# A gate/up unit's seventh product listed between the next unit's second and third products

## The chip, the cores and the metric

The kernel runs on one NeuronCore of a Trainium2 chip. The metric is device time in microseconds (us), the time of one execution on that core. The shown time of the kernel before is the median of three runs. One further execution was profiled, and every trace row in this document comes from such a profiled execution.

The engines are named as in the profile: PE is TensorE's matmul, PEld its weight load, DVE is VectorE, ACT is ScalarE, POOL is GpSimd, SP is SyncE, which issues the loads here. ACT and DVE each have one queue of instructions.

## The reference

The program is a trunk of two layers over 512 tokens of width 1024. Layer 0 mixes tokens by a stick-breaking attention, layer 1 by a gated MLP over positions. After each mixer stands a SwiGLU feed-forward part with 2816 hidden channels, and only this part matters here:

```
def swiglu(h, w_gate, w_up, w_down):
    return (jax.nn.silu(h @ w_gate) * (h @ w_up)) @ w_down
```

Everything is float32, and norms, shifts, scales and gates stand around each part.

## The kernel before

**Precision.** Each operand of a float32 product is split into a high part and a low remainder. `mm3` (L105) makes one product of two split operands from three matmuls: high by high, high weights by low activations, low weights by high activations. So in the trace `r<-hTh,wh`, `r<-hTl,wh` and `r<-hTh,wl` are the three matmuls of one step. `split` (L113) makes the two parts: ACT copies the high part (L117) and DVE subtracts it for the low part (traced as L70, since all DVE calls but those of plain weights go through a wrapper; those have L162).

**The gate/up stage.** The hidden width is 22 blocks of 128 channels. `units` (L1136) computes them for each of the two feed-forward parts: blocks 0 to 2 by plain sums (`unit`, L1065), and blocks 3 to 21, 19 of them, by `seven` (L1089). A seven unit takes gate and up of its block, two halves of the tokens (lo, hi) and two halves of the 1024 inner channels as a 2x2 by 2x2 block product, and computes it with seven block products in place of eight. Each product is 4 steps of `mm3`, so 12 matmuls of 128x128 weights by 256 tokens; a unit has 84. The products and what reads them, in the order of the listing:

| product | operands | accumulates in | then |
|---|---|---|---|
| 1 | A11 (hT), B11 | R1, fresh | ACT copies R1 to s1 (L1112) |
| 2 | A12 (hT), B21 | R2, fresh | DVE: gate lo = R2 + s1 |
| 3 | S1, T1 | R3, fresh | ACT copies R3 to s5 (L1116) |
| 4 | S2, T2 | R1, added | ACT copies R1 to u1 (L1118) |
| 5 | S4, B22 | R3, added | DVE: up lo = R3 - u1 |
| 6 | S3, T3 | R1, added | DVE: up hi = s5 - R1 |
| 7 | A22 (hT), T4 | R1, added | ACT: Silu of gate lo in place (L1126), Silu of R1 to gate hi (L1127); DVE: act = gate * up |

Row 7 of the table is the inner function `rest` (L1124), which `seven` returns. Product 7 adds into the same bank R1 that "up hi" has just read, so its first matmul has to wait for that DVE instruction. In the trace that instruction is `gu<-e,r`, and "gate lo" and "up lo" are `gu<-r,e`. A12 by B21 is seen as `r<-hTh,b` and `r<-hTl,b`, products 3 to 6 are `r<-Sh,wh`, `r<-Sl,wh`, `r<-Sh,wl`, and products 1 and 7 are both `r<-hTh,wh`, `r<-hTl,wh`, `r<-hTh,wl`.

**Weights.** `wget` (L235) hands out the next unit's weights and first emits the loads and splits of those up to one unit further. `block_loads` (L175) loads 512 KB for rawx and 512 KB for rawy; `blocks` (L186) splits them into x (holding B11, B22), b (B21), t13 (T1, T3) and t24 (T2, T4), with the sums f13 and f24 made by DVE. The split tiles live in six places, three to a unit, so the tiles of unit f+2 take over the places of unit f: its t24 can be split only when product 7 of unit f has read the old one. f24 has one buffer, f13 and b have two. The matmul banks of tag "b" are six, three to a unit.

**What orders the work.** In this stage no order is written out by hand. The listing goes to a scheduler that makes each engine's order at compile time: of the instructions that it reckons ready it takes the one that stands earliest in the listing. Each engine then runs its own order without skipping. So a place in the listing is a rank, not a place on the engine.

**Beside the units** a background generator (`Bg`, L335) loads rows of a modulation matrix and adds them up on DVE, one step (`bg0.step(1)`) after two of each three units, seen as `G<-rawada,sc,G`; its end is two 512-wide matmuls for each half of a row, `adaps`. After the stage, part 0 goes on to the down projection (`out_proj`, matmuls `y`) and part 1 to `last` (matmuls `X`, `Y`, `Z`, `W`).

Of the kernel before, what the change touches and what calls it, by code (L numbers as in the profile page):

```python
# [31 lines left out]
def trunk(ctx: ExitStack, tc: tile.TileContext, A: dict, out: bass.AP):  # L32
# [17 lines left out]
    def nm(s):  # L50
        uid[0] += 1
        return f"{s}_{uid[0]}"

    def slot(dt, name, a=2, b=512):
        return s4.tile([P, a, b], dt, tag="s4", name=nm(name))

    def bank(name, tag="b"):
        return psum.tile([P, 512], F32, tag=tag, bufs=6 if tag == "b" else 2, name=nm(name))
# [46 lines left out]
    def mm3(o, lh, ll, rh, rl, start, stop):  # L105
        mm(o, lh, rh, start, False)
        mm(o, lh, rl, False, False)
        mm(o, ll, rh, False, stop)
# [126 lines left out]
    def wget(src, look=3):  # L235

        n = taken[0]
        taken[0] += 1
        while len(got) < min(n + 1 + look, len(stream)):
            wemit()  # L240
        assert stream[n][3] == src, (stream[n][3], src)
        return got[n]
# [176 lines left out]
    def hB(hT, k, lo, n):  # L419

        h, l = hT[lo // 256, k // 4]
        lo %= 256
        return h[:, k % 4, lo : lo + n], l[:, k % 4, lo : lo + n]
# [630 lines left out]
    class Ffn:  # L1054
# [31 lines left out]
        def first(self):  # L1086
            return [lambda f=f: self.unit(f, 0, 256, 2) for f in range(NH)]

        def seven(self, f):  # L1089

            W = wget(("blocks", (self.li, f - NH)), 1)
            R1, R2, R3 = [bank(n)[:, :256] for n in ("r1", "r2", "r3")]
            S = {n: (lambda k, t=self.S[n]: (t[0][:, k, :], t[1][:, k, :])) for n in "1234"}
            S["A11"] = lambda k: hB(self.hT, k, 0, 256)
            S["A12"] = lambda k: hB(self.hT, k + 4, 0, 256)
            S["A22"] = lambda k: hB(self.hT, k + 4, 256, 256)

            def product(o, a, b, start, stop):
                for k in range(4):
                    h, l = S[a](k)
                    wh, wl = W[b](k)
                    mm3(o, wh, wl, h, l, start and k == 0, stop and k == 3)

            e = fpool.tile([P, 3, 256], F32, tag="e", name=nm("e"))
            gu = npool.tile([P, 2, T], F32, tag="n", name=nm("gu"))
            lo, hi = slice(0, 256), slice(256, T)
            s1, u1, s5 = [e[:, i, :] for i in range(3)]  # L1110
            product(R1, "A11", "B11", True, False)
            act.activation(s1, R1, AF.Copy)  # L1112
            product(R2, "A12", "B21", True, True)
            dve.tensor_tensor(gu[:, 0, lo], R2, s1, ALU.add)
            product(R3, "1", "T1", True, False)
            act.activation(s5, R3, AF.Copy)  # L1116
            product(R1, "2", "T2", False, False)
            act.activation(u1, R1, AF.Copy)  # L1118
            product(R3, "4", "B22", False, True)
            dve.tensor_tensor(gu[:, 1, lo], R3, u1, ALU.subtract)  # L1120
            product(R1, "3", "T3", False, False)
            dve.tensor_tensor(gu[:, 1, hi], s5, R1, ALU.subtract)

            def rest():  # L1124
                product(R1, "A22", "T4", False, True)
                act.activation(gu[:, 0, lo], gu[:, 0, lo], AF.Silu)  # L1126
                last_act[0] = act.activation(gu[:, 0, hi], R1, AF.Silu)  # L1127
                if f // 2 == len(self.act):
                    self.act.append(slot(F32, "act"))
                dve.tensor_tensor(  # L1130
                    self.act[f // 2][:, f % 2, :], gu[:, 0, :], gu[:, 1, :], ALU.mult
                )

            return rest

        def units(self, bg0):  # L1136
            for f in range(NH):
                self.unit(f, 256, 256)()
            for f in range(NH, KF):
                self.seven(f)()  # L1140
                if f % 3:
                    bg0.step(1)
            bg0.step(99)

        def run(self, bg0, bg, bg2, steps, nhT, nxt, nS=None):
            self.units(bg0)
# [5 lines left out]
        def last(self, bg0):  # L1152
# [102 lines left out]
            for q in range(2):  # L1255
# [4 lines left out]
                for n, p in enumerate(PAIRS[q]):  # L1260
                    W = wget(("wdn", q, p), 2)
                    now = O
                    if n + 1 < NF or q == 0:
                        O = operands(*((q, PAIRS[q][n + 1]) if n + 1 < NF else (1, PAIRS[1][0])))
                    if p in SEVEN[q]:
                        seven(now, W, banks, fresh)
                        if p == [i for i in PAIRS[q] if i in SEVEN[q]][-1]:
                            us = common(banks)
                    elif q == 1 and n >= NF - NLAST:
                        tail.append((p, now, W))  # L1270
                    else:
                        for s in range(2):
                            eight(p, now, W, banks, s, (0, 1), ("X", s) in fresh)
                            fresh -= {("X", s), ("Y", s)}
                    if q == 1 and n == NF - NLAST - 2:
                        sqrt_table()
                        xs = [x_load(tt) for tt in range(NT)]
# [277 lines left out]
```

## Time and profile before

| | us |
|---|---|
| three runs | 1136.39, 1134.57, 1135.93 |
| their median | 1135.93 |
| the profiled execution, its own time | 1133.95 |
| its span, from the first to the last instruction | 1132.2 |
| mean granted TensorE clock, as a share of full speed | 0.998 |

| engine | busy us | instructions |
|---|---|---|
| PE | 1110.9 | 7436 |
| PEld | 999.9 | 7436 |
| DVE | 933.0 | 1223 |
| ACT | 596.6 | 985 |
| POOL | 29.5 | 53 |

A timeline row reads: start in us from the span's start, duration in us, engine, line, operation, output and inputs by tile name, shapes, and how many records were merged; in brackets the idle time before it and what ended it. A row of grouped instructions ends with the count, the busy time, the mean duration in ns, and the idle time before. The end of a matmul is modelled and overlaps the next one, so the distance between two starts is what a matmul costs; a stall shows as a longer distance, often without any bracket. The seven units of part 0 stand at about 314 to 507 us, those of part 1 at about 818 to 1012 us.

### The profile page before, as it was taken

What the parts mean: (1) busy time and instruction counts of PE and PEld (TensorE: products, weight loads), DVE (VectorE), ACT (ScalarE), POOL (GpSimd) and SP (SyncE); (2) the same over time, 40 slices, a digit from 0 to 9 for tenths busy, and PEclk for the clock granted to TensorE, in tenths of its full rate; (3) what the DMA queues carried; (4) which work ended last, traced back from release to release, by engine and by line L of the source; (5) the groups of instructions that cost most, each with busy time, mean ns of one, the idle gap of its engine ahead of it and who ended that gap; (6) DMA issues with size and microseconds to landing.
All of it is one profiled execution on the core that took longest, in us unless ns stands there. A gap on an engine that the chain in (4) does not pass through costs nothing.

```text
span 1132.2 us, 18659 instructions
## 1 busy us (share of the span) xinstructions
PE 1110.9 (98%) x7436; PEld 999.9 (88%) x7436; DVE 933.0 (82%) x1223; ACT 596.6 (53%) x985; POOL 29.5 (3%) x53
## 2 busy tenths in 40 slices
PE   6999999999999999999999999999999999999997
PEld 4787878788999999998888988988999999999996
DVE  4988999958989898778686865759979898789996
ACT  6445655656655555572153624537455555465752
POOL 0120100000000000010000100001000000000000
PEclk9999999999999999999999999999999999999999
DMA  8876434214344343348886483324243434223242
GB/s 322 336 238 213 147 98 134 93 59 158 122 150 131 128 151 117 129 136 310 269 275 218 150 280 110 131 94 160 83 132 115 164 130 146 70 85 99 90 154 106
DMA packets 51356, 176.39 MB, mean 156 GB/s; under 512 B 6074, under 2 KB 9146, under 8 KB 51268
## 3 DMA queue, kind: packets, MB, share of 16 engines
q1 hardware_dynamic: 48708, 166.81, 43.6%
q0 software_dynamic: 2560, 8.39, 2.0%
q8 instruction: 58, 0.95, 0.3%
q14 instruction: 30, 0.25, 0.1%
HBM read 164.69 MB, written 8.39 MB: 153 GB/s over the span
## 4 chain that ended last, share of the span: by engine, by line
PE 88%; DVE 5%; ACT 3%; DMA 2%; issue 1%; SPq 0%; DVEq 0%; ACTq 0%
PE r L94 32%; PE y L94 16%; PE v L94 8%; PE pqk L94 7%; PE X L94 4%; PE gu L94 4%; PE Y L94 3%; PE u L94 3%; PE av L94 2%; PE z L94 2%; PE tw L102 1%; PE Z L94 1%; PE W L94 1%; PE tp L102 1%; PE ab L94 1%
## 5 line engine op out<-in xcount | busy, mean ns | idle before, releaser
L94 PE MATMUL r<-Sh,wl 128*128 128x256 f32 x608 | 170.0, 280 | 0.0
L94 PE MATMUL r<-Sh,wh 128*128 128x256 f32 x608 | 169.9, 279 | 0.0
L94 PE MATMUL r<-Sl,wh 128*128 128x256 f32 x608 | 169.8, 279 | 0.0
L161 ACT ACTIVATE wh<-raw 128x1024 fp32r<-128x1024 f32 x87 | 91.6, 1059 | 113.3 <-PE y L94 57.5
L94 PE MATMUL y<-wh,as 128*128 128x512 f32 x480 | 150.7, 391 | 0.0
L117 ACT ACTIVATE wh<-f 128x1024 fp32r<-128x1024 f32 x87 | 92.3, 1061 | 91.3 <-PE r L94 66.4
L70 DVE TENSOR_TENSOR wl<-f,wh 128x1024 fp32r<-128x1024 f32 x87 | 106.4, 1222 | 38.9 <-ACT wh L117 38.8
L162 DVE TENSOR_TENSOR wl<-raw,wh 128x1024 fp32r<-128x1024 f32 x87 | 105.8, 1221 | 38.2 <-ACT wh L161 37.5
L94 PEld LDWEIGHTS r<-Sl,wh 128*128 128x128 f32 x608 | 114.2, 188 | 0.0
L94 PEld LDWEIGHTS r<-Sh,wl 128*128 128x128 f32 x608 | 114.2, 188 | 0.0
L94 PEld LDWEIGHTS r<-Sh,wh 128*128 128x128 f32 x608 | 114.1, 188 | 0.0
L94 PEld LDWEIGHTS y<-wh,as 128*128 128x128 f32 x480 | 90.1, 188 | 18.6
L94 PE MATMUL y<-wl,as 128*128 128x512 f32 x240 | 93.8, 391 | 0.0
L94 PE MATMUL r<-hTh,wh 128*128 128x256 f32 x304 | 88.9, 293 | 0.6 <-DVE gu L70 0.6
L94 PE MATMUL r<-hTl,wh 128*128 128x256 f32 x304 | 84.8, 279 | 0.0
L94 PE MATMUL r<-hTh,wl 128*128 128x256 f32 x304 | 80.0, 279 | 0.0
L94 PEld LDWEIGHTS r<-hTh,wh 128*128 128x128 f32 x304 | 57.0, 188 | 5.9 <-DVE gu L70 2.4
L94 PE MATMUL r<-hTh,b 128*128 128x256 f32 x304 | 59.8, 279 | 0.0
L117 ACT ACTIVATE wh<-rawx 128x1024 fp32r<-128x1024 f32 x38 | 40.3, 1061 | 33.4 <-PE r L94 30.8
L94 PEld LDWEIGHTS r<-hTl,wh 128*128 128x128 f32 x304 | 57.2, 188 | 0.1
L94 PEld LDWEIGHTS r<-hTh,wl 128*128 128x128 f32 x304 | 55.0, 188 | 0.0
L94 PE MATMUL gu<-hTh,wh 128*128 128x256 f32 x192 | 54.0, 281 | 0.0
(272 smaller groups left out, 2960.7 us busy)
## 6 DMA issues: line engine op xcount, KB each, us to landing
rawada<-in_ada SPq DMA_DIRECT2D x80, 512.0 KB, 4.9
rawy<-in_wy SPq DMA_DIRECT2D x38, 512.0 KB, 3.5
rawx<-in_wx SPq DMA_DIRECT2D x38, 512.0 KB, 4.1
raw<-in_wdown SPq DMA_DIRECT2D x22, 512.0 KB, 4.6
raw<-in_wdn SPq DMA_DIRECT2D x22, 512.0 KB, 3.5
raw<-in_wqk SPq DMA_DIRECT2D x16, 512.0 KB, 4.5
ada<-in_ada0p SPq DMA_DIRECT2D x12, 512.0 KB, 9.0
raw<-in_wgu SPq DMA_DIRECT2D x12, 512.0 KB, 3.5
```

The costliest lines, as they stand in the source:

```text
L70: b = getattr(nc.vector, op)(*args, **kw)
L94: b = nc.tensor.matmul(o, l, r, start=start, stop=stop, skip_group_check=True)
L102: last_tp[0] = nc.tensor.transpose(o, i, ident)
L117: act.activation(hi, src, AF.Copy)
L161: act.activation(h[:], raw[:], AF.Copy)
L162: last_low[0] = nc.vector.tensor_tensor(l[:], raw[:], h[:].bitcast(F32), ALU.subtract)
```

## The change

`seven` takes the previous unit's `rest` as an argument and calls it after its own second product and the "gate lo" sum. `units` hands each `rest` to the next unit and calls the last one itself, after the background generator has been run out.

```diff
-        def seven(self, f):
+        def seven(self, f, pending=None):
...
             product(R2, "A12", "B21", True, True)
             dve.tensor_tensor(gu[:, 0, lo], R2, s1, ALU.add)
+            if pending is not None:
+                pending()
             product(R3, "1", "T1", True, False)
...
+            rest = None
             for f in range(NH, KF):
-                self.seven(f)()
+                rest = self.seven(f, rest)
                 if f % 3:
                     bg0.step(1)
             bg0.step(99)
+            rest()
```

No instruction is added or removed. In the listing, product 7 of a unit, its two Silus and its DVE multiply now stand behind the weight work that the next unit's `wget` emits and behind the next unit's products 1 and 2.

## The prediction

> **What bounds the kernel now.** I read the page first: busy times, then the chain that ended last.
>
> ```profile
> span 1132.2 us, 18659 instructions
> PE 1110.9 (98%) x7436; PEld 999.9 (88%) x7436; DVE 933.0 (82%) x1223; ACT 596.6 (53%) x985; POOL 29.5 (3%) x53
> PE 88%; DVE 5%; ACT 3%; DMA 2%; issue 1%; SPq 0%; DVEq 0%; ACTq 0%
> L94 PE MATMUL r<-hTh,wh 128*128 128x256 f32 x304 | 88.9, 293 | 0.6 <-DVE gu L70 0.6
> L94 PE MATMUL r<-hTl,wh 128*128 128x256 f32 x304 | 84.8, 279 | 0.0
> ```
>
> PE is busy 98% of the span and carries 88% of the chain, so a nanosecond won or lost in its order reaches the end unless another engine takes over. The last two rows are a hint: both have 304 matmuls of one size, and those that open products 1 and 7 average 293 ns against 279, so some of them are far longer. Idle time names the cause, a DVE instruction `gu`, but shows only 0.6 us of it. So next I read the timeline of PE and DVE around one unit's end.
>
> ```profile
> 333.31 0.28 PE L94 MATMUL r<-hTh,wh 128*128 128x256 f32 x1
> 333.42 0.28 PE L94 MATMUL r<-hTl,wh 128*128 128x256 f32 x1
> 333.61 0.39 PE L94 MATMUL r<-hTh,wh 128*128 128x256 f32 x1
> 333.84 0.28 PE L94 MATMUL r<-hTl,wh 128*128 128x256 f32 x1
> 332.00 1.22 DVE L70 TENSOR_TENSOR wl<-rawx,wh 128x1024 fp32r<-128x1024 f32 x1 [0.33 <-ACT wh L117]
> 333.15 0.41 DVE L70 TENSOR_TENSOR gu<-e,r 128x256 f32<-128x256 f32 x1
> ...
> 336.67 0.28 PE L94 MATMUL r<-Sh,wh 128*128 128x256 f32 x1
> 342.21 0.28 PE L94 MATMUL r<-Sh,wl 128*128 128x256 f32 x1
> ```
>
> Three things stand here. First, the order on PE is not that of the listing: at 333.42 product 1 of the next unit is still running, its twelfth matmul is missing, and at 333.61 product 7 of the old unit begins. The scheduler has already put 11 matmuls of the next unit ahead of product 7. Second, that isn't enough: "up hi" ends at 333.15 + 0.41 = 333.56, behind a weight remainder on DVE's queue, and product 7 starts 0.05 us later. Third, the price. The last two rows are the first and the last of the 48 matmuls of products 3 to 6: (342.21 - 336.67) / 47 = 0.1179 us each. From 333.42 to 333.84 are two steps, 0.42 us where 0.24 is due: **0.18 us a unit**, part waiting, part the slow first matmul after it (0.39 us long, and 0.23 to the next start).
>
> **The sum.** I take the distance from one unit's product 2 to the next one's, over each part of the network: the first and last of 19 starts, and the two stretches between them.
>
> ```profile
> 315.10 0.28 PE L94 MATMUL r<-hTh,b 128*128 128x256 f32 x1
> 325.18 0.28 PE L94 MATMUL r<-hTh,b 128*128 128x256 f32 x1
> 496.52 0.28 PE L94 MATMUL r<-hTh,b 128*128 128x256 f32 x1
> 819.40 0.28 PE L94 MATMUL r<-hTh,b 128*128 128x256 f32 x1
> 1001.11 0.28 PE L94 MATMUL r<-hTh,b 128*128 128x256 f32 x1
> ...
> 315.10:496.52 181.42, 181.19 (x1516) 178.88 (x1515) 154.09 (x206) 97.32 (x163) 0.00 (x0) 1.00 0.39 128
> 819.40:1001.11 181.71, 181.50 (x1517) 179.27 (x1515) 152.74 (x204) 97.13 (x163) 0.00 (x0) 1.00 0.37 122
> ...
> 503.59 0.40 PE L94 MATMUL adaps<-acch,ones 128*128 128x512 f32 x1
> 504.06 0.39 PE L94 MATMUL y<-wh,as 128*128 128x512 f32 x1
> ```
>
> A unit takes 325.18 - 315.10 = 10.08 us. Without a wait it is 84 x 0.1179 = 9.90. Each stretch holds 18 units and one pair of `adaps` matmuls (504.06 - 503.59 = 0.47 us), so 178.2 + 0.47 = 178.7 us would do. Saved: 181.42 - 178.7 = 2.7 us and 181.71 - 178.7 = 3.0 us, together **5.7 us** if no unit waits any more. The granted clock is 1.00 in both, so there is nothing to win or lose there.
>
> **Does the wait really go?** Product 7 will stand behind 24 matmuls of the next unit in place of 11 or 12, so it starts 12 x 0.118 = 1.41 us later against "up hi". The latest "up hi" among the steady units of part 0 is in a unit that happens to show half of the change already:
>
> ```profile
> 352.28 0.28 PE L94 MATMUL r<-Sh,wl 128*128 128x256 f32 x1
> 353.56 0.42 DVE L70 TENSOR_TENSOR gu<-e,r 128x256 f32<-128x256 f32 x1
> 353.81 0.28 PE L94 MATMUL r<-hTh,b 128*128 128x256 f32 x1
> 354.05 0.37 PE L94 MATMUL r<-hTh,wh 128*128 128x256 f32 x1
> 354.25 0.28 PE L94 MATMUL r<-hTl,wh 128*128 128x256 f32 x1
> 383.01 0.41 DVE L70 TENSOR_TENSOR gu<-e,r 128x256 f32<-128x256 f32 x1
> 383.48 0.39 PE L94 MATMUL r<-hTh,wh 128*128 128x256 f32 x1 [0.21 <-DVE gu L70]
> ```
>
> Product 6 starts its last matmul at 352.28 and "up hi" ends at 353.98, 1.70 us later; product 7 follows at 354.05 behind 14 matmuls. With 24 it would be due at 352.28 + 25 x 0.118 = 355.23, so 1.25 us remain. At 383.01, where the wait is longest, "up hi" ends at 383.42; product 7 stands behind 8 matmuls there and would come 17 steps after the start at 382.99 (quoted below), at 384.9. Both are covered. A wait already met costs nothing that I can see: products 3 to 6 have three such hand-overs to ACT and back, and their 48 matmuls run at an even 0.118.
>
> **What moves with it, and what hides it.** The step issues 12 matmuls, two Silus, one DVE multiply, no DMA; POOL and SP get none of it. It is listed behind the next `wget` (two loads on SP, four splits on ACT, their remainders and sums on DVE). Its own output `act` isn't read before the stage ends. What waits for product 7 is the split of t24 for the unit after next:
>
> ```profile
> 335.22 1.06 ACT L117 ACTIVATE wh<-f 128x1024 fp32r<-128x1024 f32 x1 [1.83 <-PE r L94]
> 336.18 0.37 ACT L1127 ACTIVATE gu<-r 128x256 f32<-128x256 f32 x1
> 338.28 0.38 ACT L1116 ACTIVATE e<-r 128x256 f32<-128x256 f32 x1 [0.90 <-PE r L94]
> 336.31 1.23 DVE L70 TENSOR_TENSOR wl<-f,wh 128x1024 fp32r<-128x1024 f32 x1 [1.62 <-ACT wh L117]
> 338.99 0.68 DVE L70 TENSOR_TENSOR f<-f,rawx 128x512 f32<-128x512 f32 x1
> L70 DVE SCALAR_TENSOR_TENSOR G<-rawada,sc,G 128x1024 f32<-128x1024 f32 x8 | 10.2, 1278 | 0.0
> ```
>
> It moves by 1.41 - 0.18 = 1.23 us. On ACT the high part and the Silu behind it then end at 336.55 + 1.23 = 337.78, before s5 is due at 338.28; without that cover s5 would be late, but product 5, its reader, starts only a product (1.4 us) after product 3. On DVE the remainder ends at 337.54 + 1.23 = 338.77, just before 338.99, when f24's one buffer is rewritten. The tile itself is needed by product 4 two units on, after 348, nine us later. Bank R1 comes free at 337.78, with the next units' first claim on it after 342. I cost all of this at nothing; the cover is thinnest on DVE (below).
>
> At the stage's end the last `rest` has no next unit:
>
> ```profile
> 504.98 0.39 PE L94 MATMUL y<-wl,as 128*128 128x512 f32 x1
> 505.53 0.39 PE L94 MATMUL r<-hTh,wh 128*128 128x256 f32 x1 [0.16 <-DVE gu L70]
> 505.75 0.28 PE L94 MATMUL r<-hTl,wh 128*128 128x256 f32 x1
> 1009.56 0.39 PE L94 MATMUL X<-wl,ah 128*128 128x512 f32 x1
> 1009.96 0.39 PE L94 MATMUL r<-hTh,wh 128*128 128x256 f32 x1
> ```
>
> There 0.77 - 0.35 = 0.42 us is lost in part 0 and some 0.28 in part 1. Both stay; at best -0.7, at worst one more remainder of 1.22 us ahead of each "up hi", +2.4. I take 0, as the `adaps` pair already stands ahead of product 7 there. After the stage PE goes straight on with `y` and `X`, so a stage that ends sooner moves all that follows.
>
> Sum, on the profiled execution: 1133.95 - 5.7 = 1128.2 (span 1126.5). The median of the runs stands 2.0 above it, so the forecast is 1135.93 - 5.7 = **1130.2 us**.
>
> **Rivals.**
>
> *The place on PE doesn't change.* The before kernel shows that the listing is only a rank. If the scheduler still puts product 7 at the end of product 1, the trace is as it was: 1135.9. Against it, product 2 ran right behind product 7 in the units that I read, so its inputs were there, and it now ranks higher. In part: if a third of the waits stay, 1132.
>
> *DVE becomes late: slower.* DVE works off its queue in order: "up hi" at 333.15 had its operands since product 6 ended near 332.4 and stood behind the remainder from 332.00. The t24 remainder comes 1.23 us later now, and in the old order everything up to "up hi" follows it, from 336.31 to 343.64 (the next row of `gu<-e,r` starts 10.08 later, at 343.23). So "up hi" would end at 344.87. Product 7 would be due at 342.21 - 0.18 + 25 x 0.118 = 344.98: just in time. But with one background step of 1.28 us in that queue it is 1.2 us late, and a restart costs 0.11 more. The last row quoted above counts 8 such steps in the first stretch, so some 16 in both: 16 x 1.3 = 21 us lost, 5.7 won, 1151 at worst; if DVE, idle 1.62 us before that remainder now, makes up half, 1141. It decides from the point where "up hi" ends more than 2.95 us after product 6's last start; the latest steady unit shows 1.70. Against it: DVE is busy 154.09 of 181.42 us, and in the longer idle time before the t24 remainder the scheduler has "gate lo" and f13 to run. On this the Trainium skill, "TensorE: Matmul & The Clock Gate", Architectural detail, says that ACT and DVE queues are strictly first in, first out; the trace agrees with 333.15.
>
> *PE falls into a faster step.* After three of the waits PE ran faster until the next one:
>
> ```profile
> 374.04 0.28 PE L94 MATMUL r<-hTl,wh 128*128 128x256 f32 x1
> 382.99 0.28 PE L94 MATMUL r<-hTl,wh 128*128 128x256 f32 x1
> ```
>
> These are 79 steps in 8.95 us, 0.1133 each. If a part kept that throughout, 18 units of 84 would save 18 x 84 x 0.0046 = 7.0 us more: 1123; both parts, 1116. Against it: each part starts at 0.118, and only a wait was seen to change it. The same page, Back-to-back issue gap, gives columns / 2.4 GHz + 2.5 ns as the isolated distance, 109 ns here. By that estimate 3192 matmuls would save 28 us and the time be some 1102; products 3 to 6, which wait for nothing, measure 117.9, so the measurement stands against it.
>
> **How the numbers follow.** Forecast (nearly all waits go, 1128 to 1132): 0.67. Part of them go (1132 to 1133.6): 0.07. Faster step: 0.04. No change: 0.09. Slower by DVE or by a new order that I don't foresee at the stage's end: 0.13. Some 0.2%, 2.3 us, is what a measurement here can tell from no change. So faster 0.78, same 0.09, slower 0.13. The range of 8 in 10 takes in the forecast, the partial case and no change: 1127.0 to 1136.5; the forecast's own range is 1128 to 1132.
>
> **What would show it.** In the timeline product 7 stands behind all twelve matmuls of product 2, the steady unit is 9.90 us, the two stretches are 178.7 us, and `r<-hTh,wh` averages near 280 ns. "up hi" ends before product 7 is due. It is wrong if a wait on `gu` remains in the steady units, if PE waits for ACT's s5 or u1, or if stages other than this one change their length by over a microsecond.

## The result

| | runs | median us | lowest to highest |
|---|---|---|---|
| before | 5 | 1135.89 | 1133.98 to 1136.39 |
| after | 5 | 1156.35 | 1153.22 to 1158.86 |

After over before: **1.0174**, 95% interval 1.0151 to 1.0196. The change costs some 20 us where the prediction had it save 5.7, and the time lies 20 us above the range.

The page of the changed kernel first: span, busy time, the chain that ended last, and three groups.

```profile
span 1154.5 us, 18593 instructions
PE 1113.3 (96%) x7436; PEld 1000.7 (87%) x7436; DVE 934.6 (81%) x1223; ACT 601.3 (52%) x985; POOL 29.5 (3%) x53
PE 52%; DVE 22%; DMA 15%; issue 6%; ACT 4%; SPq 0%; DVEq 0%; ACTq 0%
...
L94 PE MATMUL r<-Sh,wh 128*128 128x256 f32 x608 | 170.9, 281 | 2.6 <-ACT e L1118 2.0
L94 PE MATMUL r<-hTh,wh 128*128 128x256 f32 x304 | 87.0, 286 | 11.4 <-DVE gu L70 11.4
L70 DVE TENSOR_TENSOR f<-rawx,rawy 128x1024 f32<-128x1024 f32 x38 | 46.5, 1224 | 53.7 <-DMA rawx<-in_wx 52.6
```

The work is the same: the same counts, and DVE busy 934.6 us against 933.0. What changed is the chain. PE carried 88% of it and now carries 52%; DVE went from 5% to 22%, DMA from 2% to 15%. The groups say where. The wait that the change was to remove has grown: `r<-hTh,wh` idles 11.4 us for DVE's `gu`, against 0.6. And a DVE group that never idled before, the sum f13 (`f<-rawx,rawy`), waits 53.7 us in 38 instructions, nearly all of it for the load of rawx. In the kernel before its row is:

```profile
L70 DVE TENSOR_TENSOR f<-rawx,rawy 128x1024 f32<-128x1024 f32 x38 | 46.3, 1220 | 0.0
```

Next, which stage lost the time. These are the busy times by stretch: the two gate/up stages with the down projection of part 0 between them, first of the kernel before, then of the changed one. The first column after the colon is the length of the stretch, then PE's and PEld's busy time with counts, DVE's and ACT's; the granted clock is third from the end.

```profile
313.69:506.93 193.24, 192.84 (x1607) 189.90 (x1605) 165.39 (x223) 108.47 (x183) 2.87 (x3) 1.00 0.40 131
506.93:630.90 123.97, 123.89 (x553) 101.63 (x552) 97.18 (x108) 45.26 (x72) 2.56 (x4) 1.00 0.75 256
817.99:1011.37 193.38, 193.15 (x1607) 190.28 (x1606) 163.69 (x219) 105.39 (x174) 0.00 (x0) 1.00 0.37 123
```

```profile
314.53:514.07 199.54, 192.49 (x1606) 189.51 (x1605) 163.92 (x221) 109.08 (x180) 2.88 (x3) 1.00 0.38 122
514.07:645.58 131.51, 126.98 (x553) 103.74 (x552) 99.32 (x110) 46.76 (x76) 2.57 (x4) 0.97 0.74 245
832.98:1033.09 200.11, 193.22 (x1607) 190.48 (x1605) 163.71 (x218) 107.74 (x174) 0.00 (x0) 1.00 0.36 116
```

The gate/up stages lose 199.54 - 193.24 = 6.3 and 200.11 - 193.38 = 6.7 us, and the down projection, which the change doesn't touch, 131.51 - 123.97 = 7.5. Together 20.6 of the 1154.5 - 1132.2 = 22.3 us by which the two profiled spans differ. So there are two losses to explain.

**Inside the gate/up stage.** First PE in the timeline of the changed kernel: three starts of product 2, and the end of a product 2 further on.

```profile
324.42 0.28 PE L94 MATMUL r<-hTh,b 128*128 128x256 f32 x1
364.00 0.28 PE L94 MATMUL r<-hTh,b 128*128 128x256 f32 x1
375.06 0.28 PE L94 MATMUL r<-hTh,b 128*128 128x256 f32 x1
...
386.32 0.28 PE L94 MATMUL r<-hTh,b 128*128 128x256 f32 x1
388.19 0.38 PE L94 MATMUL r<-hTh,wh 128*128 128x256 f32 x1 [1.59 <-DVE gu L70]
```

From 324.42 to 364.00 are four units, 9.895 us each: the steady unit that the prediction forecast. The next takes 375.06 - 364.00 = 11.06. At 388.19 product 7 stands, as intended, right behind the last matmul of the next unit's product 2, and still waits 1.59 us for "up hi". So the order on PE is the forecast one, the first units run as forecast, and then "up hi" comes too late. Why, DVE's timeline in the same unit shows (some rows are left out).

```profile
374.83 1.22 DVE L70 TENSOR_TENSOR wl<-rawx,wh 128x1024 fp32r<-128x1024 f32 x1
375.96 0.42 DVE L70 TENSOR_TENSOR gu<-e,r 128x256 f32<-128x256 f32 x1
...
382.04 1.22 DVE L70 TENSOR_TENSOR f<-rawx,rawy 128x1024 f32<-128x1024 f32 x1 [3.59 <-DMA rawx<-in_wx]
383.19 1.22 DVE L70 TENSOR_TENSOR wl<-f,wh 128x1024 fp32r<-128x1024 f32 x1
384.32 0.69 DVE L70 TENSOR_TENSOR act<-gu 128x512 f32<-128x512 f32 x1
...
386.58 1.22 DVE L70 TENSOR_TENSOR wl<-rawx,wh 128x1024 fp32r<-128x1024 f32 x1
387.72 0.42 DVE L70 TENSOR_TENSOR gu<-e,r 128x256 f32<-128x256 f32 x1
```

In the kernel before, the prediction's row at 336.31 has the t24 remainder (`wl<-f,wh`), and 338.99 is the first half of f24; f13 comes behind both, and the next remainder of x behind that:

```profile
339.59 1.22 DVE L70 TENSOR_TENSOR f<-rawx,rawy 128x1024 f32<-128x1024 f32 x1
342.08 1.23 DVE L70 TENSOR_TENSOR wl<-rawx,wh 128x1024 fp32r<-128x1024 f32 x1 [0.34 <-ACT wh L117]
```

Here f13 stands *ahead* of the t24 remainder, at 382.04, and DVE sits idle 3.59 us before it, for rawx. Everything behind it is late: the remainder, `act`, f24, the remainder of x at 386.58, and "up hi" at 387.72. f13 has moved ahead like this in 25 of the 36 places where it can (12 of 18 in part 0, 13 of 18 in part 1); in the first units of each part, which run as forecast, it has not. Three pieces of the chain that ended last give the other half of the story.

```profile
376.08 5.84 DMA rawx<-in_wx
387.83 2.97 DMA rawx<-in_wx
398.32 4.73 DMA rawx<-in_wx
```

The load is issued at 376.08, 0.03 us after the remainder of x ends (374.83 + 1.22 = 376.05), since that instruction is the last to read the buffer. So the load waits for DVE's x, f13 waits for the load, and the next x waits for f13 in the queue: a **closed loop**. Around it: 5.84 for the load and 387.83 - 381.92 = 5.9 from landing to the end of the next x on DVE, 11.75 us against the 9.9 that PE needs. With a shorter load the next turn takes 398.32 - 387.83 = 10.5. The kernel before has the same loop, but with room in it: there, from the start of f13 to the end of the next remainder of x are 342.08 + 1.23 - 339.59 = 3.7 us, here 386.58 + 1.22 - 382.04 = 5.8, since the t24 remainder, `act` and the first half of f24 now stand in between. Units that hold no wait cannot make up for it, because behind the first one no unit of the changed kernel takes less than 9.89.

**In the down projection** PE's timeline of the changed kernel has one large wait.

```profile
588.30 0.40 PE L94 MATMUL y<-wh,as 128*128 128x512 f32 x1
592.13 0.80 PE L94 MATMUL adaps<-accl,ones 128*128 128x512 f32 x1 [3.43 <-DVE accl L70]
592.72 0.63 PE L94 MATMUL y<-wh,as 128*128 128x512 f32 x1
593.15 0.63 PE L94 MATMUL y<-wl,as 128*128 128x512 f32 x1
```

`adaps` are the closing matmuls of the background generator that runs in this stage. PE waits 3.43 us for a split of its row, `accl`; over the whole stretch it idles 131.51 - 126.98 = 4.5 us. Behind the wait a matmul takes 593.15 - 592.72 = 0.43 us to the next start, where 0.23 is usual, until about 598: the granted clock of 0.97 in this stretch is that.

### The profile page after: what moved, and what is told of

It reads as the page before. It is cut to its first block, busy times and chain, and to the rows that moved or that the text cites. A ratio compares the mean times of both kernels' runs of the same rounds, so it can differ in the third digit from the quotient of the medians.

```text
span 1154.5 us, 18593 instructions
## 1 busy us (share of the span) xinstructions
PE 1113.3 (96%) x7436; PEld 1000.7 (87%) x7436; DVE 934.6 (81%) x1223; ACT 601.3 (52%) x985; POOL 29.5 (3%) x53
## 4 chain that ended last, share of the span: by engine, by line
PE 52%; DVE 22%; DMA 15%; issue 6%; ACT 4%; SPq 0%; DVEq 0%; ACTq 0%
PE r L94 11%; PE y L94 9%; DMA rawx<-in_wx 8%; PE v L94 8%; PE pqk L94 7%; DVE wl L70 6%; DMA rawada<-in_ada 4%; PE gu L94 4%; DVE f L70 3%; PE u L94 3%; PE av L94 2%; PE z L94 2%; DVE wl L162 2%; PE tw L102 1%; DVE gu L70 1%
## 5 line engine op out<-in xcount | busy, mean ns | idle before, releaser
L94 PE MATMUL r<-hTh,wh 128*128 128x256 f32 x304 | 87.0, 286 | 11.4 <-DVE gu L70 11.4
L70 DVE TENSOR_TENSOR f<-rawx,rawy 128x1024 f32<-128x1024 f32 x38 | 46.5, 1224 | 53.7 <-DMA rawx<-in_wx 52.6
L94 PE MATMUL r<-hTh,wl 128*128 128x256 f32 x304 | 84.8, 279 | 0.0
```

The source lines that it names most:

```text
L70: b = getattr(nc.vector, op)(*args, **kw)
L94: b = nc.tensor.matmul(o, l, r, start=start, stop=stop, skip_group_check=True)
```

## The experiments

**The theory** after reading the traces. (1) The later split of t24 left a gap on DVE in the scheduler's reckoning, and f13 was put into it, ahead of the remainder; there it waits for a load that DVE itself holds back. (2) The down projection is late because the generator's chain of additions starts later against the end of the stage than before. **The rivals**: product 7's place by itself makes "up hi" or its readers late, whatever DVE's order; the last `rest` after the generator's end in the listing is what hurts; the generator is paced by its own loads.

Each kernel starts from the changed one unless said otherwise. `order(a, b)` puts instruction a behind b on their common engine, without a wait.

### The old order on DVE, product 7 kept in its new place

```diff
+    last_f24 = [None]
...
-        dve.tensor_tensor(
+        b13 = dve.tensor_tensor(
             f13[:]...
+        if last_f24[0] is not None:
+            order(b13, last_f24[0])
...
-        dve.tensor_tensor(f24[:, 0:4, :], f13[:, 0:4, :], xr[:, 4:8, :], ALU.add)
+        last_f24[0] = dve.tensor_tensor(f24[:, 0:4, :], f13[:, 0:4, :], xr[:, 4:8, :], ALU.add)
```

> The changed kernel with one order added on DVE: the sum f13 of a block (it reads the freshly loaded rawx) stays behind the first half of f24 of the block before, as it stood before the change. Product 7 keeps its new place. Theory (load loop): in the changed kernel f13 stands ahead of the t24 remainder and waits there for rawx, whose buffer DVE itself frees only one remainder and two short sums earlier; with f13 behind, the wait is covered and both gate/up stages run at 9.9 us a unit: about 1130 us, or about 1138 if the 7.5 us lost in the down projection of part 0 have a cause of their own. Rival (the later t24 remainder itself makes DVE late): the order of f13 matters little, 1150 to 1156.

Measured: 1134.89 us (10 runs, 1131.09 to 1138.74), ratio to before 0.9997 (0.9981 to 1.0014). DVE's timeline around a unit, and the three stretches:

```profile
378.42 1.23 DVE L70 TENSOR_TENSOR wl<-f,wh 128x1024 fp32r<-128x1024 f32 x1 [1.15 <-ACT wh L117]
...
380.16 0.69 DVE L70 TENSOR_TENSOR f<-f,rawx 128x512 f32<-128x512 f32 x1
380.76 1.22 DVE L70 TENSOR_TENSOR f<-rawx,rawy 128x1024 f32<-128x1024 f32 x1
...
383.97 0.42 DVE L70 TENSOR_TENSOR gu<-e,r 128x256 f32<-128x256 f32 x1
```

```profile
315.06:505.12 190.06, 190.06 (x1607) 189.42 (x1606) 164.30 (x221) 110.70 (x179) 2.87 (x3) 1.00 0.40 128
505.12:633.57 128.45, 125.75 (x553) 102.82 (x552) 99.35 (x110) 46.86 (x76) 2.57 (x4) 0.99 0.75 251
820.47:1010.49 190.02, 190.02 (x1607) 189.59 (x1606) 163.66 (x218) 109.18 (x174) 0.00 (x0) 1.00 0.38 123
```

f13 stands behind the remainder and the first half of f24 again, in every unit, and its waits come to 0.2 us in all. In both gate/up stages PE is busy for the whole stretch (190.06 of 190.06). They are 193.24 - 190.06 = 3.2 and 193.38 - 190.02 = 3.4 us shorter than before: **6.5 us**, where the prediction had 5.7. So the wait does go, and the 9.5 and 10.1 us that the changed kernel loses against this one there are DVE's order alone. Yet the program isn't faster: the down projection takes 128.45 us against 123.97, and 4.5 of the 6.5 us are given back. There PE has the wait of the changed kernel in small:

```profile
581.28 0.50 PE L94 MATMUL adaps<-accl,ones 128*128 128x512 f32 x1 [2.61 <-DVE accl L70]
...
582.21 0.63 PE L94 MATMUL adaps<-acch,ones 128*128 128x512 f32 x1
582.64 1.05 PE L94 MATMUL y<-wh,as 128*128 128x512 f32 x2
```

2.61 us of waiting, and matmuls 0.43 us apart behind it, which add 125.75 - 123.89 = 1.9 us to PE's busy time.

### Product 7 one product earlier

`pending()` is called after product 1 and its copy to s1, ahead of product 2.

> The changed kernel with product 7 listed one product earlier, between the next unit's first and second. Theory (load loop): the t24 remainder is ready as early as before the change, f13 stays behind it, no load is waited for; and product 7 stands behind 12 matmuls in place of 11, which is just past the end of up hi in the trace of before (333.66 against 333.56), so most of the 0.18 us a unit goes: 1130 to 1134. Rival (any later place of product 7 costs): between 1136 and 1156.

Measured: 1133.16 us (10 runs), ratio 0.9969 (0.9956 to 0.9982). DVE keeps the order of before without any hand. The stages are 191.1, 127.4 and 189.6 us long; with twelve matmuls less of delay, f13 isn't moved ahead in any unit. In the down projection PE again waits, 2.0 us at 581, and the second theory doesn't hold for this kernel: the generator's first addition starts at 502.63, 4.5 us ahead of the last gate/up matmul at 507.17, just as in the kernel before.

### The new order on DVE, product 7 in its old place

The kernel before, with one thing forced: the t24 remainder stands behind the f13 of the block two units on.

```diff
+    lows = []
...
+        if len(lows) % 19 > 1:
+            order(lows[-2], b13)
...
-        split(t24[0][:], t24[1][:], f24[:])
+        act.activation(t24[0][:], f24[:], AF.Copy)
+        lows.append(dve.tensor_tensor(t24[1][:], f24[:], t24[0][:].bitcast(F32), ALU.subtract))
```

> The kernel before, product 7 not moved, with only the order on DVE forced: each t24 remainder behind f13 of the block two further on, as in the changed kernel. Theory (load loop): f13 meets an unfinished load in each unit, the loop of load (some 5 us) and DVE work from f13 to the remainder that frees the buffer (5.5 to 7.5 us) sets the unit's time, 10.6 to 12.6 us: 1155 to 1230. Rival (product 7's own move is what costs): 1134 to 1142.

Measured: 1167.39 us (2 runs), ratio 1.0281 (1.0247 to 1.0314); the gate/up stages take 210.8 and 205.4 us. The group of f13 on the page:

```profile
L70 DVE TENSOR_TENSOR f<-rawx,rawy 128x1024 f32<-128x1024 f32 x38 | 46.5, 1224 | 39.7 <-DMA rawy<-in_wy 38.4
```

The order alone costs as much as the change and more, and it is forced in 34 of the 36 places, against 25 in the changed kernel; here the load that f13 waits for is that of rawy, whose buffer DVE frees as well. With this the four cases are filled:

| | t24 remainder ahead of f13 | f13 ahead of t24 remainder |
|---|---|---|
| product 7 in its old place | 1135.9 | 1167.4 |
| product 7 behind the next product 2 | 1134.9 | 1156.4 |

Down the left column the move of product 7 changes little; along the rows the order costs 31.5 and 21.5 us.

### The load taken away

To test the loop from its other side: DVE's order as in the changed kernel, rawx loaded for the first block of each part only.

```diff
+    one = [None]
...
-        x = wraw.tile([P, KD, P], F32, tag="raw", name=nm("rawx"))
+        if idx[1] == 0:
+            one[0] = wraw.tile([P, KD, P], F32, tag="raw", name=nm("rawx"))
+            load(one[0][:], A["wx"][idx])
+        x = one[0]
...
-        load(x[:], A["wx"][idx])
```

> The changed kernel, but rawx is loaded only for the first block of each part and kept, so that the later blocks use the first one's rawx weights (part of the computation is changed). f13 still stands ahead of the t24 remainder in most units. Theory (load loop): without the load there is nothing to wait for, the gate/up stages take 190 us each in place of 199.5 and 200.1, 1134 to 1139. Rival (the later t24 remainder makes DVE late by itself): the stages stay near 200, 1154.

Measured: 1134.44 us (one run). The same group, and f13 still ahead of the t24 remainder (`wl<-f,wh` follows at 377.26):

```profile
L70 DVE TENSOR_TENSOR f<-rawx,rawy 128x1024 f32<-128x1024 f32 x38 | 46.5, 1223 | 10.3 <-DMA rawy<-in_wy 8.4
```

```profile
375.51 1.23 DVE L70 TENSOR_TENSOR f<-rawx,rawy 128x1024 f32<-128x1024 f32 x1 [1.23 <-DMA rawy<-in_wy]
...
377.26 1.22 DVE L70 TENSOR_TENSOR wl<-f,wh 128x1024 fp32r<-128x1024 f32 x1
```

The stages take 190.2 and 190.3 us. f13 is ahead in 30 of the 36 places, more than in the changed kernel. So the bad order does no harm when the load of rawx isn't in the loop: both parts are needed. The run has 512 KB less to load in each unit, so the other loads may land sooner too; that isn't separated. A third buffer for rawx might break the loop as well; it wasn't tried.

### The last unit's place in the listing

`rest()` of the last unit is called ahead of `bg0.step(99)` in place of behind it.

> The changed kernel with the last product 7 of a stage listed ahead of the background generator's end, as before the change. If the 7.5 us that the down projection of part 0 lost come from that place in the listing: about 1149. If they come from the gate/up stage being late or from its order on DVE: 1156 as the changed kernel.

Measured: 1159.29 us (2 runs), ratio 1.0209 (1.0183 to 1.0236); stages 200.4, 130.1 and 201.6 us. The down projection is 1.4 us shorter than in the changed kernel and still 6.1 longer than before, and nothing is won in all: that rival falls.

### What the down projection gives back

Six kernels on the second loss. The first addition of that stage's generator is `A<-rawada,sc,A`; it starts at 502.39 before, with the last gate/up matmul at 506.93, and at 504.22 in the first experiment, with the last one at 505.12. That is 4.5 us ahead of the stage's end, and 0.9.

*The generator's first load earlier*: the first experiment, with the fifth weight load of the down projection (number 4) held on SP behind the generator's first load.

> f13 pinned as before, and on SP the fifth load of the down projection's weights pinned behind the small load that the background generator's first row (A) starts from, as it stood before the change. In the run with f13 alone pinned, both gate/up stages were 190.0 us as forecast, but the down projection of part 0 took 128.5 us for 124.0, with PE waiting 2.6 us for the generator's last row and then running at half clock for some 3 us. Theory (the generator started 3.6 us late because its row load stood behind one more weight load on SP): the first addition moves from 0.9 us to some 4.5 us ahead of the stage's end, the wait goes, down projection 124 to 125 us, about 1130. Rival (the generator's own pace of load and addition is the limit): the wait stays, 1134.

Measured: 1137.1 us (10 runs), ratio 1.0002 (0.998 to 1.0024), the down projection 130.9. The addition stayed 0.9 us ahead of the end, since its place on DVE had not moved: the edit missed what it aimed at and says nothing of the theory. PE's waits there came to 2.6 us for `as` and 1.2 for `accl`.

*The generator's closing matmuls later*: the first experiment, with those matmuls listed one weight row later, `mid` +2 in place of +1 in `out_proj`.

> f13 pinned, and in the down projections that carry the generator its closing matmuls are put one weight row later (after row 14 in place of 13, so 5.5 us later on PE). Theory (PE waits there for the generator): the wait of 2.6 us and the half clock behind it go, the down projection takes 124 us, about 1130. Rival (the loss in the down projection has another cause): 1134 as with f13 alone pinned.

Measured: 1132.69 us (10 runs), ratio 0.9971 (0.9951 to 0.9992). The down projection takes 126.4, PE's wait is 1.4 us: between the theory and its rival.

*The same one edit in the kernel before.*

> Control: the kernel before with only the generator's closing matmuls one weight row later. Its trace shows no wait there, but no room either (0.3 us), so 1133 to 1136; if it gains as much as the pinned kernel does, what e6 gains isn't owed to the change.

Measured: 1137.4 us (10 runs), ratio 1.0013 (0.9996 to 1.003). Alone it wins nothing: the down projection takes 124.5 us, and the mixer behind it 191.4 where it was 187.1.

*The generator's first step listed ahead of the last product 7*, on the first experiment (and weight load 2 on SP behind the generator's first load):

```diff
-        def units(self, bg0):
+        def units(self, bg0, ahead=None):
...
+            if ahead is not None:
+                ahead.step(1)
             rest()
...
-            self.units(bg0)
+            self.units(bg0, bg)
```

> The pinned version (f13 held behind the previous block's f24) with one more edit at the end of part 0: the first step of the background generator that runs beside the down projection is listed ahead of the last unit's product 7, and the third weight load of the down projection (number 2) stands on SP behind that generator's first load. Theory A (the down projection loses its 4.5 us because the generator's first addition falls 0.94 us ahead of that stage's end in place of 4.54 us, and its chain of additions has no slack): the first addition comes back to 4 to 5 us ahead of the last product, PE's wait on accl near 581 us goes from 2.6 us to under 0.5, the down projection of part 0 takes 124 to 125.5 us, and the time is 1129 to 1132. Rival B (the chain is paced by its own loads, whenever it starts): the first addition comes back but the wait stays at 2 us or more, the down projection takes 127 to 130, and the time is 1133 to 1136. Both expect the r stages at 190.0 us.

Measured: 1132.97 us (12 runs), ratio 0.9975 (0.9962 to 0.9989). The addition starts 3.1 us ahead of the stage's end, not 4 to 5; the wait on `accl` is 1.2 us, between the two theories, and the stage takes 127.4, in B's range. Neither holds in full.

*Both of these together.*

> The run before this one, with the generator's closing matmuls listed one weight row later in the down projection as well. Theory A (a wait of PE on the generator's chain is all that the down projection of part 0 loses): a row more of cover takes up whatever wait the run before left; no PE wait over 0.3 us near 580 us, the down projection at 123.5 to 125 us, the time 1128 to 1130.5, below the kernel before. Rival B (what is lost there is not that wait): the wait goes but the stage stays at 126 to 128 and the time at 1132 to 1134.

Measured: median 1132.62 us (12 runs, 1117.53 to 1136.31) against 1135.57 for the kernel before beside it. The down projection takes 126.8 us; there is a wait of 1.6 us left at 581, now ended by ACT's copy `yp`. These are B's figures for time and stage, though B had the wait gone.

*Product 7 behind product 1, closing matmuls one row later.*

> Product 7 listed behind product 1 of the next unit alone (DVE's order then stays as in the kernel before) and the generator's closing matmuls one weight row later. Theory A (wait of 2.0 us on accl at 581 us, with half clock behind it, is what this place still gives back): the wait goes or falls under 0.5 us, the down projection of part 0 takes 124 to 125.5 us against 127.4, the time is 1130 to 1131.5. Rival B (the row later only shifts the wait): 126.5 to 127.5 us there, and 1132.5 to 1134.

Measured: **1131.41 us** (12 runs, 1130.35 to 1136.0), ratio 0.9971 (0.9958 to 0.9984), by the median the fastest version of all, though its ratio can't be told from the 0.9969 of the same kernel without the later closing matmuls. Its stretches of the down projection and of the mixer behind it, then the wait there and the load in its chain:

```profile
506.71:630.53 123.82, 123.73 (x553) 101.31 (x551) 97.14 (x108) 45.17 (x72) 2.57 (x4) 1.00 0.77 256
630.53:821.01 190.48, 186.10 (x1211) 168.19 (x1209) 135.81 (x177) 92.11 (x150) 5.04 (x8) 0.99 0.44 145
```

```profile
686.29 0.50 PE L94 MATMUL v<-wh,hTh 128*128 128x512 f32 x1 [2.49 <-ACT vt L1354]
```

```profile
680.52 4.58 DMA rawy<-in_wy
...
685.12 0.02 ACT b L117
...
685.66 0.59 ACT vt L1354
```

A holds for the down projection: no wait, 123.8 us, what it took before. But then the next stage is 190.5 us long where it was 817.99 - 630.90 = 187.1 before. PE waits for ACT's `vt`, and the chain behind it is a load of rawy that lands at 685.10, with the copy of b and then `vt` behind it on ACT. So this edit moves a loss as much as it removes one. The kernel before with the same edit has a wait for `vt` there too, 1.8 us, and the 191.4 us above, with its gate/up stages as they were; so the loss in the mixer needn't be owed to a faster gate/up stage.

**What stays open.** With the first experiment's order the down projection never came below 126.4 us. For the version behind product 1 it was shown that PE's wait on the generator is what that stage loses, by taking the wait away; what makes the generator's chain end late wasn't shown. From the first addition to the last one ahead of the closing matmuls are 69.4 us before, 68.6 in the first experiment, 71.0 behind product 1 and 70.3 with the start moved. So in the first experiment the late start can account for the wait; behind product 1, where the start is as early as before, the longer chain can; and with the start moved ahead by 2.2 us the chain became 1.7 us longer, so that only 1.1 was won. That is reckoned from the traces and not tested. What stretches the chain seems to be the rival, the generator's own loads: in the changed kernel 59.1% of the chain that ended last between 514 and 594 us is loads of rawada, issued when an addition has freed a buffer, a second loop of load and DVE. What makes these loads longer in one kernel than in another stays open.

## Why the prediction was wrong

**What bounds the kernel, and the sum: right.** The wait on "up hi" was there, the unit without it is 9.89 us (forecast 9.90), and with DVE's order held 6.5 us went (forecast 5.7). Product 7 stands behind all twelve matmuls of product 2, and a wait that is already met costs nothing: in the first experiment PE is busy throughout. One sign was set wrong: after the change the stretch from the first product 2 to the last holds one product 7 less, so it is due at 178.7 - 12 x 0.118 = 177.3 us and not 178.7; the first experiment has 177.1 in both parts.

**The step that failed** is "What moves with it, and what hides it", which ends in "I cost all of this at nothing; the cover is thinnest on DVE". It moved the t24 split by 1.23 us and then read the rest of DVE's queue from the trace of before, in the order of before. But that order was made at compile time from the scheduler's reckoning of what is ready, and the change moves just that. In 25 of 36 places f13 of the block two units on went ahead of the later remainder and stood there waiting, 52.6 us in all for rawx, which the step had at nothing. That the scheduler saw a gap there is inferred: no trace shows its reckoning, but with product 7 only one product later than before f13 keeps its place throughout. The prediction even named that candidate, as an argument *against* a loss: "the scheduler has 'gate lo' and f13 to run". It didn't ask whether f13's inputs are there at that time. The trace of before held the answer: rawx's buffer comes free when the remainder of x ends, 332.00 + 1.22 = 333.22, f13 ran at 339.59, and the 6.4 us between cover a load that takes 3 to 6. "No DMA" was true of what the step issues and missed the load that DVE releases.

**The rival "DVE becomes late" had the place right, not the mechanism.** Its point of decision held: at 387.72 "up hi" ends 4.6 us after product 6's last start at about 383.5, past the 2.95, and product 7 waits. Its price was worked out in the old order with some 16 background steps; the first experiment has that order and those steps, and no unit waits. The loop through the load wasn't among the rivals, and "a new order that I don't foresee" stood only "at the stage's end" and shared 0.13 with the slow DVE. The end of the range at 1136.5 followed from that. Three of the prediction's own signs of being wrong were there: the wait on `gu`, a wait for ACT's s5 (L1118 in the changed kernel, 2.0 us on the page), and another stage longer by 7.5 us.

**"A stage that ends sooner moves all that follows" failed too.** In the first experiment 6.5 us won became 0.6 in the profiled span (1131.6 against 1132.2): 4.5 went in the down projection, and the rest in stretches that differ by a microsecond or so from run to run. Even with the right order on DVE the forecast of 1130.2 would have been some 5 us low.

**The end of part 0 and the place on PE** were right as far as they went: moving the last `rest` back in the listing won nothing.

## What to carry to other kernels

In a kernel whose queues are ordered by a scheduler, moving one step re-orders the others: before a neighbour is priced by its old place, ask which instruction the scheduler can pull into the gap and whether its inputs have landed by then. An instruction that frees a load buffer, the load, and a reader of that load on the same queue form a loop; its length (load plus queue from reader to releaser) must stay under the period of the stage. A gain in one stage is booked only when the next stages keep their length: one with a background chain paced by loads can take it back.

## What the runs showed of the chip

**Half clock after short waits.** Between 300 and 1120 us of these traces PE's matmuls fell to half speed (0.43 us a start in place of 0.23, a granted clock of 0.50) for some 3 to 6 us behind single waits of 1.8, 1.9, 2.0, 2.1, 2.5, 2.6, 3.4 and 4.1 us, and behind none of 1.7 us or less. One wait of 2.6 us, at 580.12 in the run with the load taken away, was not followed by it, so the length of the wait alone doesn't decide. The Trainium skill, "TensorE: Matmul & The Clock Gate", What's actually happening, has the half clock follow at least one idle window of about 3.4 us. These runs agree on the half, but waits of 1.8 and 1.9 us were enough here.

**A faster step that comes and goes with a wait.** In the experiment with the closing matmuls later on the first experiment's order, part 1 ran its first seven units at the prediction's faster step. A wait ahead of that part, two starts of product 2, and the place where the step ends:

```profile
799.08 0.33 PE L102 MATMUL tp<-identt,t 128*128 128x128 f32 x1 [0.93 <-DVE t L70]
...
840.13 0.28 PE L94 MATMUL r<-hTh,b 128*128 128x256 f32 x1
849.65 0.28 PE L94 MATMUL r<-hTh,b 128*128 128x256 f32 x1
...
893.18 0.38 PE L94 MATMUL r<-Sh,wh 128*128 128x256 f32 x1
893.40 0.28 PE L94 MATMUL r<-Sl,wh 128*128 128x256 f32 x1
```

A unit takes 849.65 - 840.13 = 9.52 us there, and 9.52 / 84 = 0.1133 us a matmul. The matmuls run at that step from about 800 us, right behind the wait, until 893.18, where one takes 0.22 us to the next start and is 0.38 us long, as behind a short wait; the later units took 9.89 again. So here too only a wait was seen to change the step. Not every wait does: in the first experiment a wait of 0.99 us at the same place was followed by 0.118. The faster step made that stage 187.3 us in place of 190.0. All of both parts at it would save 3192 x 0.0045 = 14 us, about as far as the run at 1117.53 us stands below its median, but that run has no trace, and what decides between the steps stays open.
